# The attention stage's transfers in the program's order, with the stores of gates and outputs two dense steps later

## The chip, the cores and the metric

One core of one Trainium2 chip runs the kernel. The metric is the device time of one execution in microseconds; the smaller the better. Times are medians of several executions. The profile shows one more execution, taken by the hardware profiler. Its engines are TensorE (PE, with its weight loads PEld), VectorE (DVE), ScalarE (ACT), GpSimd (POOL) and SyncE (SP). SyncE computes nothing here; it issues the transfers (DMAs) between the chip's memory and the core's on-chip buffers.

## What is computed

One layer of an encoder over two token groups (2048 and 512 tokens, width 1024, 16 learned meta tokens ahead of each), in float32. Cut to what matters:

```python
u = rms_norm(h, norm_g)
qa, ka, va, za, qb, kb, vb, zb, ga, gb = split(u @ w_in)
o_a = neighbourhood_attention(qa, ka, va, na_rpb)      # 8 x 16 window on a grid of 64 columns, plus meta tokens
o_b = window_attention(qb, kb, vb, t5_bias, sink)      # +-128 tokens, plus meta tokens, with a sink logit
y_a = (o_a * silu(za)) @ w_proj_a
y_b = (o_b * silu(zb)) @ w_proj_b
h = h + (sigmoid(ga) * y_a + sigmoid(gb) * y_b) @ w_out
return rms_norm(h[:, N_META:], final_g)
```

Each attention has 8 heads of 64; the second one has 2 heads of keys and values. TensorE's products run in a reduced format, so each operand is split into a high and a low part and a product is made of three (`mm3`, L145 to L148).

## The kernel before, in words

The 2560 tokens are five windows of 512 (window 0 is the small group, windows 1 to 4 the large one). The kernel has three stages.

The first stage makes all projections and writes queries, keys, values, the SiLU gates (z) and most merge gates to memory on the chip's DRAM. Its TensorE and SyncE orders are written out by hand. In it there is a small delay list: `later(steps, fn, ...)` (L582) puts a call on a list, and `tick()` (L585), called after each product, counts the list down and makes the calls that are due. It is used for stores of values.

The second stage, from L1603, is attention with dense work between. A list of `units` (L1572 to L1579) holds, window by window, 32 units of grid attention (`unit_a`, L1085: four pairs of heads p, two heads h, four column groups g) and then 16 of window attention (`unit_b`, L1182: two head groups, four blocks n, two pairs i). A unit is a generator with five parts: loads, scores, normalising, transposes, product with the values. The loop at L1627 takes one step for each unit i: it makes the loads of unit i+4, the scores of i+2, the normalising of i+1, the transposes of i and the value product of i-1. Between these, `fill` (L1608) takes steps of the dense work (`phases`, L1547): the last merge gates (`last_gates`, L1297), the projections of the attention's output (`dense_pa`, `dense_pb`), the output product (`dense_out`) and the scaling of the finished rows (`scaled_out`, L1385). A dense step is usually six matmuls of 128x512.

The loads of a grid unit come when g = 0. With h = 0 they are q, the keys `kd` (a large piece from ka and a small one, kam, of the meta tokens), the values `v` and the bias `ba`. With h = 1 they are z, then kd, v and ba (L1097 to L1117). Those of a window unit are v, q and bias (`bb`, and `bb0` in the first block) at n = 0, z at n = 2, and keys `kbt` with two small meta pieces at i = 0 (L1192 to L1215). The buffers are in the pool `ld` (L1583): two each for q, z, keys and bias, three for v. A load has to wait until the last reader of its buffer's former content is done. The z tiles are read by GpSimd in the product at L1178 (grid) and L1291 (window), once all value products of the tile are done. Weights come through `Weights.next` (L234), which loads two tiles ahead (`wraw`, two buffers) and has the high and low parts made by ScalarE and, in this stage, GpSimd (L207, L208). Gates read back and residual rows go through `gated` (L1318), two ahead, with four buffers.

What sets the order: inside `tc.manual_schedule(engines={E.PE})` (L1604) TensorE runs in the program's order. For all other engines, SyncE's queue among them, a planner chooses an order at build time by a simulated timeline, and each engine then works through its instructions one after the other. A transfer at the head of SyncE's queue that waits holds all behind it.

Stores in this stage are those of the gates (`put_act`, L294: multiply, tanh, scale and shift, then store to `g_d`) and of the scaled output (L1391), which GpSimd makes ready.

The third stage is the end of the last window (`finish_end`, L1443), with TensorE and SyncE in the program's order.

## Time and profile before

| | |
|---|---|
| times of three runs | 1878.94, 1876.60, 1883.45 us |
| median | 1878.94 us |
| profiled execution, its time | 1880.83 us |
| profiled execution, its span | 1879.0 us, mean granted TensorE clock 0.997 |
| TensorE busy in the span | 1855.5 us |
| SyncE's transfers | 1336, 412.45 MB |
| DMA time of these, share of 16 engines | 68.3% |

The span goes from the first to the last instruction. A window of the trace is a stretch of the span: the first stage fills about 0 to 970 us, the attention stage about 970 to 1800 us, the end the rest. The DMA share is the mean busy share of the core's 16 DMA engines. A row of a timeline gives the start in us from the beginning of the span, the duration, the engine (SPq is SyncE's queue, where the duration is that of issuing), the line, the operation, the tiles as output<-input, the count of merged instructions, and in brackets idle time of the engine before it and what ended it. A row of waits gives who waited for whom, total us, how often, and the longest. Line 142 is the helper `move`, which issues every transfer.

### The profile page before, as it was taken

What the parts mean: (1) busy time and instruction counts of PE and PEld (TensorE: products, weight loads), DVE (VectorE), ACT (ScalarE), POOL (GpSimd) and SP (SyncE); (2) the same over time, 40 slices, a digit from 0 to 9 for tenths busy, and PEclk for the clock granted to TensorE, in tenths of its full rate; (3) what the DMA queues carried; (4) which work ended last, traced back from release to release, by engine and by line L of the source; (5) the groups of instructions that cost most, each with busy time, mean ns of one, the idle gap of its engine ahead of it and who ended that gap; (6) DMA issues with size and microseconds to landing.
All of it is one profiled execution on the core that took longest, in us unless ns stands there. A gap on an engine that the chain in (4) does not pass through costs nothing.

```text
span 1879.0 us, 29757 instructions
## 1 busy us (share of the span) xinstructions
PE 1855.5 (99%) x9755; PEld 1582.1 (84%) x9755; DVE 1317.5 (70%) x2914; ACT 1146.7 (61%) x2531; POOL 778.6 (41%) x599
## 2 busy tenths in 40 slices
PE   8999999999999999999999999999999999999998
PEld 6998888888888888888878888888888888888887
DVE  8886657556476655444458888778787877888874
ACT  6454444444365444444356797798789778878932
POOL 2015443323104232323224436657855874786420
PEclk9999999999999999999999999999999999999999
DMA  7565756645295677644259878977996897698383
GB/s 261 197 169 212 208 171 182 220 177 180 84 347 188 182 223 200 199 140 162 104 194 316 275 227 263 307 210 229 311 298 192 281 320 246 197 320 282 117 295 130
DMA packets 288146, 414.36 MB, mean 221 GB/s; under 512 B 117736, under 2 KB 162360, under 8 KB 286456
## 3 DMA queue, kind: packets, MB, share of 16 engines
q1 hardware_dynamic: 287704, 412.45, 68.3%
q8 instruction: 78, 1.28, 0.3%
q14 instruction: 76, 0.62, 0.1%
q10 hardware_dynamic: 288, 0.01, 0.0%
HBM read 303.46 MB, written 108.91 MB: 219 GB/s over the span
## 4 chain that ended last, share of the span: by engine, by line
PE 87%; DMA 7%; DVE 3%; ACT 1%; issue 1%; SPq 1%; POOL 0%; DVEq 0%; ACTq 0%
PE pa L857 23%; PE pe L857 12%; PE pc L857 6%; PE mm L147 3%; PE mm L148 3%; PE mm L146 3%; PE pso L148 3%; PE pso L146 3%; PE pso L147 3%; PE tp L1254 2%; PE tp L1152 2%; DMA kd<-ka 2%; PE psa L148 2%; PE psa L146 2%; PE psa L147 2%; PE s L1234 1%
## 5 line engine op out<-in xcount | busy, mean ns | idle before, releaser
L208 POOL TENSOR_TENSOR wt<-wraw,wt 128x512 fp32r<-128x512 f32 x164 | 212.1, 1313 | 250.6 <-ACT wt L207 250.6
L857 PE MATMUL pa<-u,wt 128*128 128x512 f32 x1008 | 242.8, 389 | 0.6 <-DVE wt L208 0.6
L857 PE MATMUL pa<-u,x 128*128 128x512 f32 x984 | 236.5, 389 | 0.0
L207 ACT CAST wt<-wraw 128x512 fp32r<-128x512 f32 x312 | 177.8, 619 | 74.6 <-PE mm L148 29.8
L857 PEld LDWEIGHTS pa<-u,wt 128*128 128x128 f32 x1008 | 188.9, 188 | 40.3 <-DVE wt L208 1.1
L857 PEld LDWEIGHTS pa<-u,x 128*128 128x128 f32 x984 | 184.6, 188 | 38.4
L826 POOL TENSOR_TENSOR s<-wraw,raw 128x512 f32<-128x512 f32 x40 | 58.3, 1456 | 276.8 <-DVE x L208 276.8
L146 PE MATMUL mm<-u,wt 128*128 128x512 f32 (+2 forms) x416 | 151.0, 363 | 7.2 <-ACT u L334 7.2
L147 PE MATMUL mm<-u,wt 128*128 128x512 f32 (+2 forms) x416 | 147.6, 355 | 1.0 <-DVE u L335 0.8
L148 PE MATMUL mm<-u,wt 128*128 128x512 f32 (+2 forms) x416 | 147.3, 354 | 0.0
L208 DVE TENSOR_TENSOR wt<-wraw,wt 128x512 fp32r<-128x512 f32 x148 | 105.6, 751 | 50.1 <-ACT wt L207 49.8
L857 PE MATMUL pe<-u,wt 128*128 128x512 f32 x504 | 121.3, 390 | 0.0
L857 PE MATMUL pc<-u,wt 128*128 128x512 f32 x504 | 121.1, 389 | 0.0
L1155 ACT CAST ph<-tp 128x384 fp32r<-128x384 f32 (+6 forms) x160 | 81.8, 511 | 55.9 <-PE tp L1152 54.4
L857 PE MATMUL pe<-u,x 128*128 128x512 f32 x480 | 115.3, 389 | 0.0
L831 POOL TENSOR_TENSOR s<-wraw,s 128x512 f32<-128x512 f32 x42 | 56.6, 1347 | 136.1 <-DVE wt L208 132.0
L1058 DVE CUSTOM_DVE_ANT_0 s<-s,ba 128x384 f32<-128x384 f32 (+5 forms) x160 | 86.8, 543 | 36.8 <-PE s L1129 26.6
L857 PEld LDWEIGHTS pc<-u,wt 128*128 128x128 f32 x504 | 94.6, 188 | 19.6
L857 PEld LDWEIGHTS pe<-u,wt 128*128 128x128 f32 x504 | 94.4, 188 | 19.6
L146 PE MATMUL pso<-mh,wt 128*128 128x512 f32 x256 | 107.6, 420 | 0.0
L1156 DVE TENSOR_TENSOR pl<-tp,ph 128x384 fp32r<-128x384 f32 (+6 forms) x160 | 94.9, 593 | 16.6 <-ACT ph L1155 13.7
L857 PEld LDWEIGHTS pe<-u,x 128*128 128x128 f32 x480 | 90.1, 188 | 18.7
(274 smaller groups left out, 5031.7 us busy)
## 6 DMA issues: line engine op xcount, KB each, us to landing
wraw<-in_w_in_dram SPq DMA_DIRECT2D x86, 512.0 KB
raw<-in_w_in_dram SPq DMA_DIRECT2D x40, 512.0 KB
q<-qa SPq DMA_DIRECT2D x40, 512.0 KB
wraw<-in_w_o_dram SPq DMA_DIRECT2D x32, 512.0 KB
kbt<-kb SPq DMA_DIRECT2D x32, 384.0 KB
qa<-evq SPq DMA_DIRECT2D x20, 512.0 KB
qb<-evq SPq DMA_DIRECT2D x20, 512.0 KB
ka<-evk SPq DMA_DIRECT2D x20, 512.0 KB
```

Source lines behind the costliest of these rows:

```text
L146: nc.tensor.matmul(ps, wh, uh, start=first, stop=False)
L147: nc.tensor.matmul(ps, wh, ul, start=False, stop=False)
L148: nc.tensor.matmul(ps, wl, uh, start=False, stop=last)
L207: high[0] = nc.scalar.copy(h, r).ins
L208: low[0] = (eng or lo_eng[0]).tensor_sub(l, r, f32(h)).ins
L826: eng.tensor_sub(s3, a11, a21)
L831: eng.tensor_sub(s4, a12, s2)
L857: nc.tensor.matmul(ps, wt[:, a, s], u[:, b, kk, :], start=first and kk == 0 and i == 0, stop=kk == 3 and i == 2, skip_group_check=True)
L1058: nc.vector.tensor_tensor_reduce(s[:, :n], s[:, :n], bias, -1.0, 3.0e38, ALU.add, ALU.min, nm)
L1152: nc.tensor.transpose(tp[:kb, i * P : (i + 1) * P], pr[:, x : x + kb], ident)
L1155: nc.scalar.copy(ph_[:kb, a], tb)
L1156: nc.vector.tensor_sub(pl_[:kb, a], tb, f32(ph_[:kb, a]))
```

## The change

SyncE gets the program's order in the attention stage too, and stores of gates and outputs in this stage are put on the delay list for two steps; each dense step now counts the list down. Before the pools of the first stage are closed, and at the end of the stage, the list is emptied. In the first stage `apart[0]` is 0, so a store is issued at once there, as before.

```diff
     mark = [None]
+    queue, apart = [], [0]
+
+    def put_out(dst, src):
+        if apart[0]:
+            later(apart[0], move, dst, src)
+        else:
+            move(dst, src)
...
             nc.scalar.activation(t, src, func)
-        move(dst, t)
+        put_out(dst, t)
...
-    queue = []
     lag = [2]
...
+    def flush():
+        while queue:
+            tick()
...
     def open_dense():
+        flush()
         last.close()
...
-        move(dst[f * P : (f + 1) * P, c0 : c0 + WTOK], hT)
+        put_out(dst[f * P : (f + 1) * P, c0 : c0 + WTOK], hT)
...
-    with tc.manual_schedule(engines={E.PE}):
+    apart[0] = 2
+    with tc.manual_schedule(engines={E.PE, E.SP}):
...
             while due >= 1 and next(dense, "end") != "end":
                 due -= 1
+                tick()
...
         for _ in dense:
-            pass
+            tick()
+        flush()
```

## The prediction

> **What bounds the kernel now.** First the page's busy times, then the windows of the attention stage, then what TensorE waits for there.

> ```profile
> PE 1855.5 (99%) x9755; PEld 1582.1 (84%) x9755; DVE 1317.5 (70%) x2914; ACT 1146.7 (61%) x2531; POOL 778.6 (41%) x599
> ```
> ```profile
> 1250.00:1300.00 50.00, 50.00 (x306) 44.00 (x305) 39.77 (x113) 43.45 (x115) 33.75 (x27) 1.00 0.66 223
> 1300.00:1350.00 50.00, 50.00 (x303) 43.34 (x302) 42.62 (x107) 37.88 (x85) 42.10 (x35) 1.00 1.00 298
> 1350.00:1400.00 50.00, 47.58 (x271) 40.63 (x270) 38.76 (x98) 40.27 (x96) 30.76 (x26) 0.97 1.03 320
> 1500.00:1550.00 50.00, 47.66 (x281) 40.45 (x280) 39.69 (x98) 39.12 (x86) 39.90 (x33) 1.00 1.03 324
> ```
> ```profile
> PE s L1128 <- DMA kd<-ka: 2.9, 2, 2.0
> PE oa L1169 <- DVE pl L1156: 0.9, 1, 0.9
> ```
> The columns of the windows are length, busy time of PE, PEld, DVE, ACT and POOL, granted clock, DMA share and GB/s. TensorE is busy for 1855.5 of 1879.0 us, and a window of the attention stage is full (50.00 of 50.00) except two, which lose 2.42 and 2.34 us. These are the two in which the DMA share passes 1.00. The first row shows the opposite: just before, a third of the DMA time is unused. The waits name the cause: keys (kd) that land late, 2.9 us in two waits from 1000 us on. So TensorE sets the time, the loads cost it a little in two places, and the change touches only when loads and stores are issued.

> The larger of these waits, in TensorE's timeline:

> ```profile
> 1353.90 0.39 PE L147 MATMUL pso<-ml,wt 128*128 128x512 f32 x1
> 1354.13 0.40 PE L148 MATMUL pso<-mh,wt 128*128 128x512 f32 x1
> 1356.54 0.41 PE L1128 MATMUL s<-kd,q 128*128 128x384 f32 x1 [2.01 <-DMA kd<-ka]
> 1358.33 0.63 PE L148 MATMUL pso<-mh,wt 128*128 128x512 f32 x1
> 1358.76 0.63 PE L146 MATMUL pso<-mh,wt 128*128 128x512 f32 x1
> ```
> Starts that were 0.23 us apart are 0.43 us apart after the wait: the clock fell. Its cost is in the window's clock, 0.97 of 50 us, so 1.5 us besides the wait of 2.0. **What can be won** is therefore small: 2.42 + 2.34 us of idle time, 1.5 us of clock and some tenths elsewhere, about 6 to 8 us, below 0.5% of 1879 us (9.4 us), which is about what a measurement of this kernel can tell from no change.

> **The change, part by part.** No instruction is added or removed on any engine; the count of transfers stays. What moves is the order of one queue, SyncE's, which works through its transfers one after the other. A transfer whose buffer is not free, or whose data is not ready, holds all behind it. In the planner's order a load that can go early goes early. In the program's order it stands behind everything that the code issues before it.

> *The stores two dense steps later.* A gate's store waits for the last operation on it (L291). Two dense steps later the gate is normally done, so the wait is short and little is held. The tile is kept some us longer, but there are four such buffers and a gate comes once in four dense steps; the same holds for the eight output tiles. Nobody reads these results soon. I cost it at 0; without the delay, each store would hold all loads behind it until its gate is done.

> *The z load ahead of the keys.* In the attention unit with g = 0 and h = 1 the code issues z first and then kd, kam, v and the bias. At the start of each window's grid attention this z takes the buffer of a z of window attention that GpSimd has to read first (L1291). The planner placed the keys ahead of that wait:

> ```profile
> 1116.26 0.32 SPq L142 DMA_DIRECT2D kd<-ka  x1
> 1116.63 0.46 SPq L142 DMA_DIRECT2D kd<-kam  x1
> 1124.94 0.32 SPq L142 DMA_DIRECT2D kd<-ka  x1
> 1141.10 0.34 SPq L142 DMA_DIRECT2D z<-za  x1
> 1141.53 0.37 SPq L142 DMA_DIRECT2D kd<-ka  x1
> ```
> ```profile
> 1139.62 1.29 POOL L1291 TENSOR_TENSOR y<-y,z 128x512 f32<-128x512 f32 x1 [5.37 <-DVE y L1288]
> ...
> 1299.34 1.28 POOL L1291 TENSOR_TENSOR y<-y,z 128x512 f32<-128x512 f32 x1
> ...
> 1468.89 1.28 POOL L1291 TENSOR_TENSOR y<-y,z 128x512 f32<-128x512 f32 x1
> ...
> 1637.06 1.28 POOL L1291 TENSOR_TENSOR y<-y,z 128x512 f32<-128x512 f32 x1
> ```
> ```profile
> 1142.59 0.29 PE L1128 MATMUL s<-kd,q 128*128 128x288 f32 x1
> ...
> 1302.50 0.33 PE L1128 MATMUL s<-kd,q 128*128 128x384 f32 x1
> ...
> 1472.29 0.33 PE L1128 MATMUL s<-kd,q 128*128 128x384 f32 x1
> ...
> 1640.16 0.30 PE L1128 MATMUL s<-kd,q 128*128 128x312 f32 x1
> ```
> Two key buffers serve the units, so the kd of 1116.26 is that of h = 0, the one of 1124.94 that of h = 1, and 1141.53 belongs to the next pair of heads. TensorE wants h = 1 at 1142.59. In the program's order it can't be issued before z, and z not before GpSimd's end at 1139.62 + 1.29 = 1140.91. From GpSimd's end to a kd behind the z are 1141.53 - 1140.91 = 0.62 us. How long kd takes is in the chain of waits:

> ```profile
> 1116.63 3.37 DMA kd<-kam
> ...
> 1344.51 11.74 DMA kd<-ka
> ```
> The pair issued at 1116.26 had landed at 1116.63 + 3.37 = 1120.00, 3.74 us after the first issue, in a queue that was nearly empty; in the full one it took 11.74. I take 3.74. The keys land at 1140.91 + 0.62 + 3.74 = 1145.27, which is 2.7 us late. By the same sum the next windows are late by 1300.62 + 4.36 - 1302.50 = 2.5, 1470.17 + 4.36 - 1472.29 = 2.2 and 1638.34 + 4.36 - 1640.16 = 2.5. Together **9.9 us**. GpSimd starts these products as soon as they can, so I see no room for an earlier release; below this the cost falls only if TensorE is already late for another reason.

> *Bytes moved into full stretches.* In windows 2 and 3 more than kd slips. In window 2 three loads of that unit went out long before the wait:

> ```profile
> 1262.70 0.35 SPq L142 DMA_DIRECT2D v<-va  x1
> ...
> 1283.60 0.41 SPq L142 DMA_DIRECT2D kd<-ka  x1
> ...
> 1286.19 0.33 SPq L142 DMA_DIRECT2D ba<-in_bias_a_dram  x1
> ```
> ```profile
> ba<-in_bias_a_dram SPq DMA_DIRECT2D x16, 640.0 KB
> ...
> v<-va SPq DMA_DIRECT2D x16, 480.0 KB
> kd<-ka SPq DMA_DIRECT2D x16, 480.0 KB
> ```
> These 1600 KB move from the window with a DMA share of 0.66 to behind 1300.6, into the one with 1.00. At its 298 GB/s they take 5.5 us. During the stall of 2.5 us the DMAs go on, so 3.0 us are left that the stretch can't absorb, since it ends in a wait for keys already. For windows 2 and 3 that is **6.0 us**. Its bounds are 0 (if everything else runs so far ahead that it is absorbed) and 2 x 5.5 = 11.

> *The first keys of window attention.* In window 0 the code issues v, two q, four pieces of bias and two of the first block's bias ahead of kbt, and all of them behind a gate's store:

> ```profile
> 1052.69 0.59 DVE L291 TENSOR_SCALAR eva<-eva 128x512 f32<-128x512 f32 x1 [0.23 <-ACT eva L290]
> ```
> ```profile
> 1050.09 2.44 SPq L142 DMA_DIRECT2D bb<-in_bias_b_dram  x4
> ...
> 1060.25 1.26 SPq L142 DMA_DIRECT2D kbt<-kbm  x2
> 1061.55 1.11 SPq L142 DMA_DIRECT2D q<-qb  x2
> ```
> ```profile
> 1060.95 0.29 PE L1234 MATMUL s<-kbt,q 128*128 128x274 f32 x1
> ```
> The gate is done at 1052.69 + 0.59 = 1053.28. Issuing costs 0.61 us for each of six pieces of bias (2.44 / 4), 1.11 for both q, 0.8 for the store and v (at the 0.4 that a kd or kam takes above): kbt is issued at 1058.85. Two more issues of 0.63 follow until its second meta piece, 1060.1, and that needs 3.37 us: 1063.5, against 1060.95, **2.5 us** late. It is 0 if the gate comes 2.5 us earlier, and about 2 us more if the bytes ahead in the queue and not the issues set the landing.

> *The clock.* Each new gap is about as long as the one in the timeline (the last start before it plus 0.23 is 1354.36, so 1356.54 - 1354.36 = 2.18 us), which cost 1.5 us of clock; the wait of 0.9 us left the clock at 1.00 in its window. I take 1.5 us for each of the four z gaps, **6.0 us**; the bounds are 0 and 7.5 (all five gaps). [...]

> **The sum.** 9.9 + 6.0 + 2.5 + 6.0 = 24.4 us. The two late waits of now stay, since the stretches that cause them get more to do. The profiled execution took 1880.83 us around its span of 1879.0, and it lies 1.9 us above the median of 1878.94. So 1880.83 + 24.4 - 1.9 = 1903.3, rounded to 1903.

> **The rivals.**

> *Faster: the late keys of 1354 come in time.* The kd of 1344.51 took 11.74 us in the full queue, and a v had been queued ahead of it:

> ```profile
> 1343.97 0.45 SPq L142 DMA_DIRECT2D v<-va  x1
> ```
> In the program's order kd goes ahead of v (480 KB, 491,520 bytes, 1.6 us at 298 GB/s), and an output's store goes two steps later. That is most of the wait of 2.0, and with it the 1.5 of the clock and the other small waits could go: 1879 less 6 to 8, about 1872. It decides if the z waits cost nothing, that is if the keys of h = 1 land before TensorE wants them in all four windows. Against it stands the sum above: they would have to come over 2 us earlier than GpSimd's end allows.

> *Slower, but the clock stays.* If the gaps don't pull the clock down, only the waits count: 1903.3 - 6.0 = 1897. For it speaks the wait of 0.9 us, which left the clock at 1.00; against it the one of 2.18, the nearest in length. [...]

> *No change: the waits are absorbed.* If the keys come less late (a shorter landing than 3.74, a later TensorE because of earlier small waits), the z gaps shrink to 1 us each, the clock stays at 1.00, and the full stretches use the pauses. Then 4 to 5 us are added and a few taken away: 1876 to 1886, about 1881. For it speaks that the DMAs have a third of their time free before the full stretches.

> *Much slower: the delayed stores hold the loads all along.* The waits of SyncE in the attention stage are long already, though a waiting transfer there holds only what the planner put behind it:

> ```profile
> SPq L142 <- POOL y L1291: 21.9, 12, 4.6
> ```
> Twelve such waits reach up to 4.6 us. If all of them, and not the four, cost 2.5 us and their clock, that is 8 x 4 = 32 us more, and the time is about 1935. Against it: in the middle of window attention a kbt is wanted less often, and z is needed there at half time only.

> *That the order does not change* is excluded: the planner issued the v of 1262.70 before the kd of 1283.60, although the code issues kd first in a unit.

> **How the numbers follow.** Forecast 0.48 (own range 1893 to 1915: the bytes between 0 and 11 and the clock between 3 and 7.5 move it by some 10 on both sides), the clock stays 0.16 (1889 to 1905), no change 0.21, much slower 0.09, faster 0.06. The range has to leave out no more than 2 in 10: from 1876, the low end of the no-change case, to 1922, which leaves out the faster case, most of the much slower one and a little of the upper tail of the forecast. Faster by over 0.5% means below 1869.5, which only a part of the faster case reaches: 0.03. Within 0.5% (to 1888.3) are the no-change case, the rest of the faster one and the lowest tail of the slower ones: 0.26. Slower is left with 0.71.

> **What would show it.** In the profile of the changed kernel, at the start of each window's grid attention, SyncE's z follows GpSimd's L1291 and the kd of h = 1 follows that z; TensorE's waits name kd at L1128 with four gaps of 2 to 3 us, near 1143, 1305, 1477 and 1650. The windows with a DMA share of 1.00 last longer, and granted clock under 1.00 shows behind the gaps. TensorE's busy work and instruction counts are as now. I am wrong if kd is issued behind z and TensorE still doesn't wait (my landing of 3.74 or the time of need is off), if the waits name values, bias or weights instead of keys, or if stores of gates head SyncE's waits.

## The result and the profile after

The changed kernel takes 1936.62 us (median of six runs, 1932.03 to 1938.72), the kernel before 1877.88 us (six runs beside them): a ratio of 1.0305, interval 1.0285 to 1.0325. It is slower by 58.7 us where 24.4 were forecast, and lies above the upper end of the range (1922). The profiled execution took 1932.03 us, the fastest of the six; its span is 1930.2, and the mean granted clock 0.991. The profiled execution before lies 3 us above its median. So the two profiles show 1930.2 - 1879.0 = 51.2 us of the 58.7, and what follows accounts for these. After the change the lines of the attention code have numbers that are higher by 10 (L1058 is L1068, L1128 is L1138, L1234 is L1244, L1291 is L1301), and the gate's last operation, L291, is L298.

Five windows of the attention stage (columns as before: PE, PEld, DVE, ACT, POOL, granted clock, DMA share, GB/s):

```profile
1050.00:1100.00 50.00, 42.81 (x244) 36.33 (x243) 34.17 (x107) 34.81 (x95) 16.37 (x13) 0.93 0.69 219
...
1250.00:1300.00 50.00, 50.00 (x306) 44.26 (x305) 38.19 (x113) 45.85 (x121) 25.50 (x20) 1.00 0.72 222
1300.00:1350.00 50.00, 46.30 (x266) 39.69 (x265) 37.36 (x98) 31.04 (x76) 34.16 (x28) 0.93 0.80 249
1350.00:1400.00 50.00, 45.44 (x264) 37.62 (x263) 37.64 (x94) 35.57 (x81) 37.33 (x31) 1.00 1.04 312
1400.00:1450.00 50.00, 46.60 (x265) 40.99 (x264) 36.18 (x100) 40.10 (x103) 21.80 (x17) 0.93 0.72 224
```

TensorE is no longer full, and most losses do not lie where the DMAs are full: of the 42.8 us that are idle in the sixteen windows from 1000 to 1800 us, 9.2 lie in the two with a DMA share of 1.00 or more, and the worst window (7.2 us idle, and a clock of 0.93) has 0.69. So most of the loss is not a lack of bandwidth. What VectorE and TensorE wait for in this stage:

```profile
DVE s L1068 <- DMA ba<-in_bias_a_dram: 26.2, 23, 2.8
```
```profile
PE s L1138 <- DMA kd<-kam: 23.2, 15, 3.7
PE s L1244 <- DMA kbt<-kbm: 13.1, 6, 5.8
...
PE s L1138 <- DMA kd<-ka: 1.4, 1, 1.4
```

Keys are late 22 times, where the forecast had five and the profile before had two of note; the bias of grid attention is late on VectorE 23 times. Before, the row of this bias read:

```profile
DVE s L1058 <- DMA ba<-in_bias_a_dram: 9.3, 5, 4.3
```

SyncE's own waits show the change best. First those of the kernel before, then those of the changed one; the thing behind the arrow is what the head of the queue waited for:

```profile
SPq L142 <- PE s L1235: 94.9, 26, 7.2
SPq L142 <- PE s L1129: 67.7, 30, 4.8
```
```profile
SPq L142 <- POOL y L1301: 128.1, 14, 14.9
SPq L142 <- POOL y L1188: 43.8, 6, 10.5
...
SPq L142 <- PE s L1245: 7.6, 10, 3.7
SPq L142 <- PE s L1139: 7.5, 6, 3.1
```

Before, the queue stood mostly at loads whose buffer TensorE was still reading in the scores: 162.6 us. That is a healthy wait, since the load goes out when its buffer is free: in the trace before, the issue ended 0.17 us after the release by the median of these 56 waits, and 0.55 at most. After, that wait is down to 15.1 us, and the queue stands at z tiles that GpSimd has not read yet, 171.9 us. When the queue comes to the keys, their buffer is mostly free already, so they go out later than they could. Worked out from the timelines of all 40 loads of each kind, the medians of the time from a load's issue to its first use are:

| load | before | after |
|---|---|---|
| bias `ba` | 10.4 us | 8.6 us |
| keys `kd` | 11.6 us | 9.6 us |
| keys `kbt` | 12.3 us | 9.1 us |

### The profile page after: what moved, and what is told of

Read it like the earlier page. It is cut to its first block, busy times and chain, and to the rows that moved or that the text cites. A ratio compares the mean times of both kernels' runs of the same rounds, so it can differ in the third digit from the quotient of the medians.

```text
span 1930.2 us, 29605 instructions
## 1 busy us (share of the span) xinstructions
PE 1870.0 (97%) x9755; PEld 1586.0 (82%) x9755; DVE 1317.9 (68%) x2914; ACT 1145.1 (59%) x2531; POOL 778.4 (40%) x599
## 3 DMA queue, kind: packets, MB, share of 16 engines
q8 instruction: 78, 1.28, 0.3%
## 4 chain that ended last, share of the span: by engine, by line
PE 73%; DMA 16%; DVE 5%; ACT 3%; SPq 1%; issue 1%; POOL 0%; DVEq 0%; ACTq 0%
PE pa L867 23%; PE pe L867 11%; PE pc L867 6%; DMA ba<-in_bias_a_dram 5%; DMA sgb<-gb 3%; PE pso L148 2%; PE pso L146 2%; PE pso L147 2%; PE mm L147 2%; PE mm L148 2%; PE mm L146 2%; PE tp L1264 2%; PE psa L146 2%; PE psa L147 2%; PE psa L148 2%; DMA kbt<-kbm 1%
## 5 line engine op out<-in xcount | busy, mean ns | idle before, releaser
L867 PEld LDWEIGHTS pa<-u,wt 128*128 128x128 f32 x1008 | 188.9, 188 | 39.8 <-DVE wt L208 0.6
L146 PE MATMUL mm<-u,wt 128*128 128x512 f32 (+2 forms) x416 | 150.8, 362 | 7.0 <-ACT u L341 7.0
L147 PE MATMUL mm<-u,wt 128*128 128x512 f32 (+2 forms) x416 | 147.0, 353 | 1.3 <-DVE u L342 1.3
L148 PE MATMUL mm<-u,wt 128*128 128x512 f32 (+2 forms) x416 | 147.0, 353 | 0.0
L1075 ACT ACTIVATE s<-s,nm 128x384 f32<-128x384 f32 (+5 forms) x160 | 87.2, 545 | 57.5 <-DVE nm L1068 55.1
L1068 DVE CUSTOM_DVE_ANT_0 s<-s,ba 128x384 f32<-128x384 f32 (+5 forms) x160 | 86.4, 547 | 38.4 <-DMA ba<-in_bias_a_dram 26.2
L146 PE MATMUL pso<-mh,wt 128*128 128x512 f32 x256 | 108.1, 422 | 0.0
```

The lines of the kernel that those rows point to most:

```text
L146: nc.tensor.matmul(ps, wh, uh, start=first, stop=False)
L147: nc.tensor.matmul(ps, wh, ul, start=False, stop=False)
L148: nc.tensor.matmul(ps, wl, uh, start=False, stop=last)
L867: nc.tensor.matmul(ps, wt[:, a, s], u[:, b, kk, :], start=first and kk == 0 and i == 0, stop=kk == 3 and i == 2, skip_group_check=True)
L1068: nc.vector.tensor_tensor_reduce(s[:, :n], s[:, :n], bias, -1.0, 3.0e38, ALU.add, ALU.min, nm)
L1075: nc.scalar.activation(out, s, AF.Exp, bias=nm, scale=-1.0, accum_out=sm)
```

## The experiments

The theory after the result: the planner issues a load as soon as its buffer allows; the code asks for it only four units ahead and behind other transfers, so in the program's order the loads lose 2 to 3 us of lead (the time from issue to first use), and a wait at the head of the queue can become a gap of TensorE. The rivals: it is the four z loads ahead of keys, and nothing else; it is all z loads, those of window attention too; it is the stores; it is the order within a unit.

Below, "idle" is TensorE's idle time from 980 us on in gaps of over 0.15 us, and "clock" what stretches at half clock cost (half their length) from 980 us to the last matmul, both added up from the trace. The kernel before has 6.1 and 1.7 us, the changed one 43.1 and 15.4: 50.7 us more, and the spans differ by 51.2.

**Order alone, delay alone.** The two parts of the change, one by one.

```diff
-    apart[0] = 2
     with tc.manual_schedule(engines={E.PE, E.SP}):
```

> SyncE in the program's order, stores of gates and outputs issued at once, not two dense steps later. Theory A (the order of the loads costs the time, and the delay of the stores protects them): each store now holds the loads behind it until its gate is done, so the time is above that of the changed kernel (1936.6 us), about 1945. Rival B (the delayed stores cost the time): the time falls well below 1936.6, to 1880 to 1905.

Measured: 1958.89 us, ratio 1.0431 (1.0414 to 1.0449), more than the 1945 that was expected.

```diff
     apart[0] = 2
-    with tc.manual_schedule(engines={E.PE, E.SP}):
+    with tc.manual_schedule(engines={E.PE}):
```

> The stores two dense steps later, SyncE's order left to the planner. Theory A: no change from the kernel before (1877.9 us), 1873 to 1883. Rival B: most of the 58.7 us of the change appear, 1910 or more.

Measured: 1877.56 us, ratio 1.0002 (0.9992 to 1.0011). So the whole loss comes from the order. The delay alone changes nothing, and beside the order it saves 22 us (1958.89 against 1936.62), because a store that is issued at once stands at the head of the queue until its gate is done: SyncE's waits for gates are 58.4 us with the order alone, 21.9 us in the changed kernel.

**z behind its unit's other loads, keys ahead of the other loads of window attention.** Each alone, and both.

```diff
-        if g == 0 and h == 1:
-            z = sh["z"] = ld.tile([P, WTOK], F32, tag="z", name="z")
-            move(z, z_d["a", w, p])
...
             move(b[:, : a_kind_width(kind)], bias_a[kind][2 * p + h])
+        if g == 0 and h == 1:
+            z = sh["z"] = ld.tile([P, WTOK], F32, tag="z", name="z")
+            move(z, z_d["a", w, p])
```

The same was done with the z of `unit_b`, behind `kbt`.

> The changed kernel with the load of z moved behind all other loads of its unit, in both attentions. Theory A: the four waits for kd at the start of the windows (2.2, 3.7, 2.5 and 2.4 us in the profile of the changed kernel) go, with the halved clock behind three of them (6.8, 3.4 and 3.4 us at half speed, 6.8 us lost), and some of the waits later in the same windows: 1905 to 1918. Rival C (the full stretches decide: every load has too short a lead, and a load that is freed only lands earlier by pushing another one back): the waits appear elsewhere, 1925 or more.

Measured: 1900.80 us, ratio 1.0124 (1.0104 to 1.0143); idle 20.9, clock 5.1. This is below the 1905 to 1918 of theory A: more than the four waits went away.

For the keys, the block `if i == 0: kt = ...` of `unit_b` with its three `move`s was put ahead of the loads of v, q and bias.

> The changed kernel with the keys of a window unit (kbt and its two meta pieces) loaded ahead of v, q and the bias; z stays where it is. Theory A: the waits for kbt (13.1 us in all, the longest 5.8, 3.4 and 2.6 us) go, with the clock behind two of them (6.8 us at half speed each, 6.8 us lost): 1914 to 1922. Rival C: the wait turns into one for q or for the bias of the same unit, 1930 or more.

Measured: 1924.01 us, ratio 1.0245 (1.0229 to 1.0261); idle 39.8, clock 8.5. This is 2 us above theory A's range: the waits for `kbt` are gone, and those for `kd<-kam` have grown from 23.2 to 28.3 us.

> The changed kernel with both moves: z behind the other loads of its unit, keys of a window unit ahead of its v, q and bias. Theory A (waits at the head of SyncE's queue): the waits for kbt left with z last (10.5 us, and 5.1 us lost to the clock) go from 1900.8: 1884 to 1890. Rival C (too short a lead in the full stretches): they turn into waits for q, bias or kd, 1894 or more.

Measured: 1892.97 us, ratio 1.0077 (1.0061 to 1.0093); idle 15.7, clock 1.7. The time lies between what the two theories gave, so this run alone does not decide between them. Both places matter, and the two edits nearly add (35.8 + 12.6 = 48.4, together 43.7). But 15 us are left, though no load stands behind a z of its own unit and keys go first.

**Which z.** Only the z of grid attention last, and only that of window attention last.

> Only the z of grid units moved behind the unit's other loads. Theory A1 (the step of the prediction: what costs is z ahead of the keys at the start of each window's grid attention): most of the 35.8 us that both moves of z gave, 1900 to 1910. Rival A2 (the long waits in the middle of window attention, up to 14.9 us, use up the lead of all loads behind them): a gain of the four waits and their clock alone, 17.6 us or less, 1919 or more.

Measured: 1906.70 us, ratio 1.0146 (1.0129 to 1.0164); idle 26.7, clock 6.8. What TensorE still waits for is keys of window attention:

```profile
PE s L1244 <- DMA kbt<-kbm: 14.8, 7, 6.1
...
PE s L1138 <- DMA kd<-kam: 4.6, 6, 1.4
```

> Only the z of window units moved behind the unit's other loads. Theory A1: little, 1928 to 1937. Rival A2: half of the 35.8 us or more, 1919 or less.

Measured: 1935.61 us, ratio 1.0313 (1.0289 to 1.0338). Putting window attention's z last gives nothing. The queue still waits 143.0 us for z tiles here (171.9 in the changed kernel), so this shows that the place of these loads in their unit does not matter; whether the waits themselves cost time is tested further below. The z of grid attention ahead of its keys costs 23.6 us of span (1930.2 - 1906.6), or 29.9 us by the medians.

**A longer lead.** z is loaded with the scores of its unit (no load of the unit stands behind it), keys go first, and most loads of grid attention (all but those of each window's first head), with those of each window's first window unit, are asked for six units ahead instead of four. The other loads of window attention stay at four.

```diff
+        LEADS, n0 = [], 0
+        for j in range(N):
+            n0 = 0 if j == 0 or units[j][:2] != units[j - 1][:2] else n0 + 1
+            far = n0 >= 4 if units[j][0] == "a" else n0 == 0
+            LEADS.append(6 if far and j >= 4 else 4)
+        ahead = 4
         for i in range(N):
...
-            if i + 4 < N:
-                next(units[i + 4][2])
+            while ahead < N and ahead - LEADS[ahead] <= i:
+                next(units[ahead][2])
+                ahead += 1
```

> Both moves taken further: z is issued with the scores of its unit (two units later than now), the keys first, and the other loads of most grid units and of a window's first window unit six units ahead and not four. Theory A: SyncE's queue gets a lead of some 5 us more where the stretches are full, and no waits for keys are left: 1872 to 1882, no slower than the kernel before. Rival C: the full stretches have no room for an earlier lead and the time stays with that of both moves, 1885 or more.

Measured: 1874.53 us, ratio 0.9979 (0.9970 to 0.9989); idle 2.1, clock 0. This is faster than both kernels, than the one before by 0.2%. It has three edits at once, so three more kernels take it apart: without the longer lead, without z at the scores, and without keys first.

> The program's order with delayed stores, keys first in window attention, and each z load issued with the scores of its unit; every other load four units ahead, as in the changed kernel. Theory A (lead: what is left at 1892.97 with z last and keys first is loads that are issued too late, and six units instead of four took the 18.4 us away): near 1893, between 1885 and 1896, with waits of TensorE for keys in window attention and of VectorE for the bias as before. Rival B (z: even behind its unit's loads a z that waits for GpSimd still holds the loads of the next units, and that was the 18.4 us): near 1876, with no wait for keys over 1 us after 1000 us.

Measured without the lead: 1899.0 us, ratio 1.0109 (1.0091 to 1.0126); 3 us above the upper end of what the lead's theory gave, and far from the 1876 of the other. SyncE's waits for z are nearly gone here (30.4 us in all, against 130.9 with z last in its unit), and the time is not better for it (idle 16.5, clock 3.4). So the z was not what was left: behind the other loads of their unit, the waits for z cost nothing that shows at this lead. What SyncE does wait for here:

```profile
SPq L142 <- PE s L1247: 106.8, 28, 7.1
...
SPq L142 <- PE s L1140: 8.3, 8, 3.0
```

The queue stands at window attention's scores again (L1247, 94.9 us before the change), but hardly at those of grid attention (L1140, 67.7 us before). The medians from issue to use say the same: the window's keys `kbt` are back at 12.5 us, the grid's `ba` and `kd` only at 9.4 and 10.9. VectorE still waits for `ba` 11 times, 21.1 us. So what is left lies mostly in grid attention, and its loads are the ones that the longer lead moves.

> The program's order with delayed stores, keys first, and the loads of most units six units ahead; z stays ahead of the keys of h = 1, as in the changed kernel. Theory A (lead): 1924.01 of the kernel with keys first alone, less 18.4 for the lead, about 1906; the gaps before the keys of h = 1 of grid attention stay, as far as z still waits for GpSimd. Rival B (z): the lead gives nothing while z is in the way, 1919 to 1926, or more, since a z that is asked for two units earlier waits for its buffer longer and holds more.

Measured with z ahead of the keys again: 1908.75 us, ratio 1.0167 (1.0144 to 1.0189). The lead gives 15 us even here (from 1924.01); the four gaps before the keys of h = 1 stay (2.17, 2.64, 2.72 and 2.57 us; idle 26.6, clock 1.7 in all).

> The kernel of 1874.53 (z with the scores, keys first, longer lead) without keys first: window attention's keys are again issued behind v, q and the bias. Theory A (lead): with two units more of lead those 3 to 5 us of issues no longer matter, 1874 to 1878. Rival C (the order within the unit matters whatever the lead): keys first was worth 1900.80 - 1892.97 = 7.8 us at a lead of four, so about 1882, with a wait for kbt at the start of window attention in window 0.

Measured: 1874.06 us, ratio 0.9983 (0.9972 to 0.9993). With the longer lead the place of the keys within the unit no longer matters; with the short one it was worth 8 to 13 us.

One late load in the kernel without the lead, in window 2: SyncE's issue, VectorE's wait for it, TensorE's wait behind that.

```profile
1360.62 0.39 SPq L142 DMA_DIRECT2D ba<-in_bias_a_dram  x1
```
```profile
1370.39 0.57 DVE L1068 CUSTOM_DVE_ANT_0 s<-s,ba 128x384 f32<-128x384 f32 x1 [3.92 <-DMA ba<-in_bias_a_dram]
...
1370.87 0.69 DVE L1167 TENSOR_TENSOR pl<-tp,ph 128x512 fp32r<-128x512 f32 x1
```
```profile
1371.61 0.33 PE L1180 MATMUL oa<-pl,v 128*64 128x256 f32 x1 [2.05 <-DVE pl L1167]
```

The bias comes 9.8 us after its issue. VectorE idles 3.92 us for it, and the operation that TensorE needs (L1167) is queued behind. TensorE's wait names VectorE, but the cause is a load. In the kernel with the longer lead VectorE has no wait for `ba`, TensorE's only wait of over 1 us after 1000 us is 1.26, and SyncE's waits and the two windows from 1300 us on are

```profile
SPq L142 <- PE s L1247: 113.0, 27, 7.1
SPq L142 <- PE s L1140: 75.8, 23, 5.8
```
```profile
1300.00:1350.00 50.00, 50.00 (x301) 43.36 (x300) 43.58 (x110) 37.97 (x87) 42.06 (x35) 1.00 0.97 315
1350.00:1400.00 50.00, 50.00 (x301) 43.87 (x300) 41.79 (x108) 44.15 (x104) 35.52 (x29) 1.00 0.85 270
```

The queue stands again where it stood before the change, at buffers that TensorE reads: 188.8 us. The medians from issue to use are back at 10.3 (`ba`), 11.7 (`kd`) and 12.6 us (`kbt`). The DMA share of the two windows also went from 0.80 and 1.04 to 0.97 and 0.85: the transfers are spread more evenly over them. How much of the gain is the earlier issue of each load and how much this evener flow was not told apart.

**The planner with the same code.** The fast kernel with SyncE's order left to the planner.

```diff
     apart[0] = 2
-    with tc.manual_schedule(engines={E.PE, E.SP}):
+    with tc.manual_schedule(engines={E.PE}):
```

> The program of 1874.53 with SyncE's order left to the planner again; only the text's order, the delay and the keys' place differ from the kernel before. If the planner places loads by when they are needed and not by where the code issues them: 1876 to 1879, as with the delay alone (1877.56), and the last 3 us come from the written order. If the planner follows the code's order where it has a choice: about 1874.5, and the written order of the queue brings nothing by itself.

Measured: 1875.19 us, ratio 0.9985 (0.9976 to 0.9995), the same as with the written order. So the written order brings nothing by itself; the 3 us come from where the code asks for loads, and the planner follows that where it has a choice.

## Why the prediction was wrong

The direction was right, and so was the step about z ahead of the keys. The step that failed is the one that kept all other loads as early as before: it put them at nothing, and they cost 14.8 us of idle time. Two terms were also too small, the first keys of window attention and the clock. The sum had 24.4 us; the profiles differ by 51.2.

| term | predicted | measured |
|---|---|---|
| z ahead of the keys | 9.9 | 10.8 |
| bytes moved into full stretches | 6.0 | 5.6 |
| first keys of window attention | 2.5 | 5.8 |
| other late loads | 0 | 14.8 |
| clock | 6.0 | 13.7 |
| sum | 24.4 | 50.7 |

**The stores two dense steps later**, costed at 0: right for the delay under the planner's order (1.0002). In the program's order it is not shown: SyncE still waits 21.9 us for gates, in seven waits, against 11.2 us in five before. The longest, 5.2 us, stands ahead of the first keys of window attention.

**The z load ahead of the keys**: right. In the changed kernel (GpSimd, SyncE, TensorE):

```profile
1150.11 1.28 POOL L1301 TENSOR_TENSOR y<-y,z 128x512 f32<-128x512 f32 x1 [5.36 <-DVE y L1298]
...
1151.42 0.32 SPq L142 DMA_DIRECT2D z<-za  x1
1151.83 0.38 SPq L142 DMA_DIRECT2D kd<-ka  x1
1152.27 0.42 SPq L142 DMA_DIRECT2D kd<-kam  x1
...
1155.45 0.37 PE L1138 MATMUL s<-kd,q 128*128 128x288 f32 x1 [2.21 <-DMA kd<-kam]
```

GpSimd ends at 1151.39, and the keys are there 4.06 us later; the prediction had 0.62 + 3.74 = 4.36. The four gaps are 2.21, 3.70, 2.54 and 2.36 us, at 1155, 1323, 1505 and 1683.

**Bytes moved**: the size agrees, the mechanism is not shown. With grid attention's z last, idle time falls from 43.1 to 26.7; less the four gaps that leaves 16.4 - 10.8 = 5.6 us, over all windows and not only in 2 and 3. The stretch from 1300 us, which was to be overfull, has a DMA share of 0.80 where it had 1.00 before, so there the DMAs had room.

**The first keys of window attention**: the place was right, the size was not.

```profile
1054.87 0.39 DVE L1068 CUSTOM_DVE_ANT_0 s<-s,ba 128x216 f32<-128x216 f32 x1 [2.23 <-DMA ba<-in_bias_a_dram]
...
1055.18 1.14 DVE L298 TENSOR_SCALAR eva<-eva 128x512 f32<-128x512 f32 x1
```
```profile
1056.34 0.33 SPq L142 DMA_DIRECT2D gb<-eva  x1
1056.76 0.39 SPq L142 DMA_DIRECT2D vb<-vb  x1
1057.19 1.08 SPq L142 DMA_DIRECT2D q<-qb  x2
1058.31 3.95 SPq L142 DMA_DIRECT2D bb<-in_bias_b_dram  x6
1062.36 0.53 SPq L142 DMA_DIRECT2D kbt<-kb  x1
1064.07 1.66 SPq L142 DMA_DIRECT2D kbt<-kbm  x2
```
```profile
1062.30 0.40 PE L148 MATMUL mm<-u,wt 128*128 128x512 f32 x1
1068.45 0.57 PE L1244 MATMUL s<-kbt,q 128*128 128x274 f32 x1 [5.76 <-DMA kbt<-kbm]
```

The gate was taken to be done at 1053.28, as before; it is done at 1055.18 + 1.14 = 1056.32, since VectorE waited for a late bias first. That is a circle: a late load delays the engine that frees the head of the queue, and the queue delays the next loads. TensorE itself comes only 1.74 us later (at 1062.69 instead of 1060.95). From the gate to the last key piece's issue are 9.41 us instead of 6.8, mostly because issues wait for earlier transfers to land (1.8 us in two waits, of a kind that the last section counts). The landing took 2.72 instead of 3.37. So 3.04 - 1.74 + 2.6 - 0.65 = 3.25 more than 2.5.

**"The two late waits of now stay"**: this step failed. The prediction took all loads but those it listed to be as early as before, and left the two existing waits as they were. (It also read all windows but two as full; those from 1050, 1100 and 1750 us lost 0.62, 0.10 and 0.51 us.) The code's lead of four units was never what made loads early; the planner was. The first bias of windows 1 to 4, for example, was issued 35 to 42 us ahead of its use before, and 10 to 13 us after. In the written order `kd`, `kbt` and `ba` lost 1.8 to 3.2 us of their 10 to 12, and 14.8 us of idle time came from places that no term had (43.1 - 6.1 - 10.8 - 5.6 - 5.8). The experiments show it as lead: without z in the way and with keys first 15 us of loss were left, moving z further did not help, and two more units of lead for the loads of grid attention took all of it. Whether each load's own earlier issue did this or the evener flow of the queue stays open.

**The clock**: 13.7 instead of 6.0. Behind the four z gaps it cost 6.8 us, near the 6.0, but by other parts: 3.4 us behind the gap at 1323 (6.83 us at half clock), 1.7 each behind those at 1505 and 1683, nothing behind that at 1155. The other 8.5 us lie behind late keys at 1068, 1407 and 1740, which had no clock term; the 1.7 us of the kernel before are gone. The windows with 0.93 hold the three stretches of 6.83 us. The 1.5 us for the stretch before came from a rounded clock (0.97 of 50 us); it is 3.41 us at half clock, so 1.7.

**The rivals.** "Much slower" gave 1935, about what was measured, by a mechanism that the runs do not bear out: it held that the delayed stores and window attention's z loads cost the time. The delay saves time in the program's order (1936.62 against 1958.89), putting these z loads last changes nothing (1.0313 against 1.0305), and at a lead of four, with keys first, the kernel with 30.4 us of z waits is no faster than the one with 130.9. It agreed by chance. "The clock stays" is refuted: the clock fell behind gaps of 2.36 and 2.54 us, for 3.41 us each. "Faster" needed the z waits to cost nothing; z ahead of the keys cost 23.6 us. "That the order does not change" is excluded by the rows of z and `kd` above. Of the signs, the four gaps came within 1 us of the forecast length except one (3.70 us); the windows with a DMA share of 1.00 did not get longer (two, where there were three).

## What to carry to other kernels

A planner that reorders a load queue hides how short the lead in the code is: before its order is replaced by the code's, compare for every load the time from its issue to its first use, and give the code that lead. In a double-buffered load queue the head should wait for the reader of the buffer that it refills; if it waits for anything else (a slower engine's tile, a store's data), all loads behind it can lose lead, and the cost appears at many places (here, with 171.9 us of waits at z tiles, the medians of lead fell by 1.8 to 3.2 us). Look at this for each kind of load: here the queue stood again at one kind's buffers for 106.8 us, at the other's for 8.3, and the time was still 1899 us. A list of the worst two collisions then gives a lower bound, not the price.

## What the runs showed of the hardware

*Waits for the transfer eight places ahead.* In the traces of the kernels before and after, the 1336 transfers of SyncE's queue use eight semaphores in turn. In the changed kernel, from 960 to 1880 us, SyncE waits 227 times for over 0.15 us for a transfer to land, and in all but one of these waits it is the transfer eight places ahead of the next one to go out. The waits take 188.2 us; SyncE's waits for transfers took 108.7 us before (137 waits) and 83.1 with the longer lead (90). So in these waits a queue that was held did not make up for it in a burst: the ninth transfer went out only when the first had landed. This is read from the trace; whether the chip or the build sets the number eight it does not tell, and the limit was not varied.
